# One token turn per tick, gains and rows asked for later, and two token operands of the FFN cut one product later

## The chip, the cores and the metric

The kernel runs on one core of one Trainium2 chip. The time is the device time of one launch in microseconds, the median of three runs. Its engines are named as the profile names them: PE (TensorE, matmuls), PEld (TensorE's weight loads), DVE (VectorE), ACT (ScalarE), POOL (GpSimd), SP (SyncE, which issues nearly all DMAs here). Each engine works through its own instructions in the order of the program and waits for the others by semaphores.

## What is computed

One layer of a decoder on 2048 tokens of 1024 float32 values (one batch): gated linear attention beside a short gated convolution, then a SwiGLU FFN of 2816 hidden values, then a gate over a per-token embedding, each behind an RMS norm and added to the residual `h`.

```python
u = _rmsnorm(h, ln1_g[i])
proj = u @ w_in[i]
q, k, v, g, g_lr, cb, cc, cx = jnp.split(proj, offsets, axis=-1)
...
mix = jnp.concatenate([o, y], axis=-1) @ w_out[i]
h = h + mix
u2 = _rmsnorm(h, ln2_g[i])
a, bb = jnp.split(u2 @ w_gate_upffn[i], 2, axis=-1)
h = h + (jax.nn.silu(a) * bb) @ w_down[i]
u3 = _rmsnorm(h, ln3_g[i])
gate = jax.nn.sigmoid(u3 @ w_ple_gate[i])
h = h + gate * (p[i] @ w_ple_proj[i])
...
return _rmsnorm(h, lnf_g)
```

`o` is the normed and gated result of the attention, `y` that of the convolution.

## The kernel before

**Number form.** A float32 operand is split into a high part (an ACT cast to fp32r) and a low part (a DVE subtraction of the high part from the source); `split_into` (L176 to L179) writes both. A product takes three matmuls for each pair of operands (high by high, high by low, low by high: `PASSES`). So each operand that comes from memory passes a DMA, an ACT cast and a DVE subtraction before PE can use it.

**Seven products for eight.** The FFN's two matmul stages and the gate of the embedding cut their matrices into 2 by 2 blocks and make seven block products in place of eight, from sums and differences of blocks. `ORDER` (1, 6, 2, 5, 7, 3, 4) is the order in which they run. The operands of the seven products (token side and weight side) are made once, stored to DRAM and loaded when their turn comes.

**Stages.** `mixing_phase` (0 to some 930 us) works on four blocks of 512 tokens: input projection, attention, convolution, output projection. The end of a block overlaps with the start of the next. Each token tile of 128 tokens is normed (`normed`: ACT squares, POOL `ms` and `rs`, DVE L212) and then *turned*: eight 128x128 PE transposes (L219) in two halves, each half into one of two PSUM banks named `tr`. There are two kinds of turn. `norm_to` turns a tile of the next block's input and splits each half into uT (ACT L178, DVE L179), and both must have read a bank before it is free. `norm_to_ops` turns a tile of the finished block for the FFN; ACT copies the halves out (L250), DMAs store them, and for blocks 1 and 3 POOL also subtracts (L234) to make operands 4 to 7.

**What sets the order around a turn.** The turns are put in a list with a due time by `later`; `tick` (L143) runs between products, and once inside a long product, and runs all entries that are due. PE's order follows from that. DVE's, ACT's and POOL's orders in this stage are made by a scheduler from the same program.

**The up stage** (`up_phase`, some 930 to 1806 us): two halves of 1024 tokens by 11 pairs of hidden chunks by seven products. `go(n, ...)` runs product n for two 128-row tiles of weights `wu` against a token operand `U[b][n]`, ticks after each tile and takes one entry of the list `side`. The token operands stay for all 11 pairs; they are loaded by `fetch_U` (L292: two DMAs into `ur`, and two cuts, each an ACT cast and a DVE subtraction into U). In the first pair the operands of products 3 and 4, the last two, are asked for after the first and second product, and their cuts go into `side` at once. The instructions of all engines are issued in the order written. `done5` adds the accumulated product to `u2` on DVE (L234 is the helper's line).

**The last phase** (`last_phase`, from some 1806 us): `down` for each half b of the tokens, then `gated` for each. `stream` (L1070) runs a product in steps of 12 matmuls; each job of two steps loads a weight operand `wr` and a token operand `mr` (`load`, L1044) and cuts them into `wh` and `mh` two jobs ahead; `load(x + 4)` is four jobs ahead. `then(n, fn)` runs `fn` n steps later. `rows_of` asks for the eight rows (`h`, 512 KB each) of the residual `h_mid`, three at once and five at step 12. `gain_of` loads a norm's gain vector to all partitions. After product 3 and 4 of `down`, each token tile is normed, turned (L1123), copied by ACT (L1124), subtracted on POOL and stored by SP (L1177) for the gate stage.

Of the kernel before, what the change touches and what calls it, by code (L numbers as in the profile page):

```python
# [19 lines left out]
NT = T // P  # L20
# [10 lines left out]
ORDER = (1, 6, 2, 5, 7, 3, 4)  # L31
GLA_WAIT = 10
EQ = 2
N1, N2, N3 = 7, 3, 3
LEVELS = (128, 64, 32, 16, 8, 4)
NL = len(LEVELS)

# [2 lines left out]
def hybrid_layer(ctx: ExitStack, tc: tile.TileContext,  # L40
# [100 lines left out]
    side = [None]  # L141

    def tick():  # L143
        clock[0] += 1
        while queue and queue[0][0] <= clock[0]:
            queue.pop(0)[1]()
        if side[0] is not None and next(side[0], "end") == "end":
            side[0] = None

# [1 line left out]
        while queue:  # L151
            queue.pop(0)[1]()

    def later(n, fn):
        queue.append((clock[0] + n, fn))
        queue.sort(key=lambda e: e[0])

    PASSES = ((0, 0), (0, 1), (1, 0))
# [63 lines left out]
    def norm_to(src, u, ti, gain, delay):  # L222
        xn = normed(src, gain)

        def transposes():
            for kk in range(2):
                tp = transposed(xn, kk)
                split_into(u[kk][:, :, 0, ti * P:(ti + 1) * P], u[kk][:, :, 1, ti * P:(ti + 1) * P], tp)
        if delay is None:
            return transposes  # L230
        later(delay, transposes)

    def tensor(e, out, a, b, op):
        return e.tensor_tensor(out=out, in0=a, in1=b, op=op)  # L234
# [1 line left out]
    def norm_to_ops(src, tile, ops, gain, delay):  # L236

        xn = normed(src, gain)  # L240
        tok = tok_of(tile % NT)
        old = w4([P, 2, 4, P]) if tile >= NT else None
        if tile >= NT:
            for kk in range(2):
                nc.sync.dma_start(out=old[:, kk], in_=ops[1 + kk][:, :, tok])

        def transposes():
            ut = w4([P, 2, 4, P])
            for kk in range(2):
                nc.scalar.copy(out=ut[:, kk], in_=transposed(xn, kk))  # L250
            put = lambda n, t: nc.sync.dma_start(out=ops[n][:, :, tok], in_=t)
            if tile < NT:
                put(1, ut[:, 0])
                put(2, ut[:, 1])
                return
            put(3, ut[:, 1])
            s = w4([P, 2, 4, P])
            g = nc.gpsimd
            tensor(g, s[:, 0], ut[:, 0], old[:, 0], ALU.subtract)
            put(5, s[:, 0])  # L260
            tensor(g, s[:, 1], ut[:, 1], s[:, 0], ALU.subtract)
            put(6, s[:, 1])
            tensor(g, ut[:, 0], ut[:, 1], ut[:, 0], ALU.subtract)
            put(7, ut[:, 0])
            tensor(g, old[:, 1], old[:, 1], s[:, 1], ALU.subtract)
            put(4, old[:, 1])
        later(delay, transposes)

    def load_x(b, ti, eng, gate=None):
        xt = w4([P, D])  # L270
# [521 lines left out]
    def up_phase(st):  # L792
# [137 lines left out]
        for b in range(NBB):  # L930
            for i in range(NPR):
                bk = {}
                s0 = 7 * (b * NPR + i)

                def go(n, on, done):

                    g = s0 + ORDER.index(n)
                    run(g)
                    w = W.pop(g)
                    bk[n] = [mm_bank() for _ in range(2)] if on is None else bk[on]  # L940
                    for e in range(2):
                        product(bk[n][e], lambda k, s: w[:, s, k, e * P:(e + 1) * P],
                                lambda k, s: U[b][n][:, k, s, :], 4, start=on is None, skip_group_check=True)
                        done(e, bk[n][e])
                        tick()
                        if side:
                            side.pop(0)()
                    if b == 0 and i == 0 and n in ORDER[:2]:
                        side.extend(fetch_U(0, ORDER[5 + ORDER.index(n)]))
                    if b + 1 < NBB and i == NPR - 1:  # L950
                        side.extend(fetch_U(b + 1, n))
                u2, b2, m1, m2 = [None] * 2, [None] * 2, [None] * 2, [None] * 2

                def done1(e, x):
                    u2[e] = v2()
                    nc.scalar.copy(out=u2[e], in_=x)  # L956

                def done2(e, x):
                    m1[e] = v2()
                    nc.scalar.activation(out=m1[e], in_=x, func=AF.Silu)  # L960

                def done5(e, x):
                    b2[e] = v2()
                    add(b2[e], x, u2[e])

                def done3(e, x):
                    m2[e] = v2()
                    add(m2[e], x, u2[e])
                    nc.scalar.activation(out=m2[e], in_=m2[e], func=AF.Silu)

                def done4(e, x):
                    add(u2[e], x, u2[e])
                    tensor(V, m2[e], m2[e], b2[e], ALU.mult)
                    tensor(V, m1[e], m1[e], u2[e], ALU.mult)
                go(1, None, done1)
                go(6, None, lambda e, x: add(u2[e], x, u2[e]))
                go(2, 1, done2)
                go(5, None, done5)
                go(7, None, lambda e, x: add(b2[e], x, b2[e]))
                go(3, 5, done3)  # L980
                go(4, 7, done4)

                put = lambda n, x, b=b, i=i: nc.sync.dma_start(out=hid_ops[b][n][:, i, :], in_=x)

                def plain(m1=m1, m2=m2, put=put):
                    put(1, m1[0])
                    put(2, m1[1])
                    put(3, m2[1])

                def sums(m1=m1, m2=m2):  # L990
                    sub(m1[0], m2[0], m1[0])
                    sub(m2[0], m2[1], m2[0])
                    sub(m2[1], m2[1], m1[0])
                    sub(m1[1], m1[1], m2[1])

                def summed(m1=m1, m2=m2, put=put):
                    put(5, m1[0])
                    put(7, m2[0])
                    put(6, m2[1])
                    put(4, m1[1])  # L1000
                at(s0 + 8, 3, plain)
                at(s0 + 8, 4, sums)
                at(s0 + 10, 3, summed)
# [5 lines left out]
    def last_phase(st):  # L1009
# [141 lines left out]
            then(start + gap[1], scale)  # L1151
            last_fn(got)

        def down(b, g3):
            h = rows_of(h_mid, b, 12)
            acc = [v("acc") for _ in range(NT)]
            bk = {}
            second = [None] * NT
# [8 lines left out]

            def complete(t, turn_at, fn):
                then(1, lambda: nc.sync.dma_start(out=h_out[b * 2 * NT + t], in_=h[t]))
                norm_steps(h[t], g3, 2 * (t % NT), (1, 3), lambda got: then(turn_at, lambda: fn(t % NT, got["xn"])))  # L1170

            def later_half(t, xn):
                second[t] = turn(xn, "ut")
# [41 lines left out]
        def rows_of(src, b, wait):  # L1215
# [4 lines left out]
                h[t] = pl["h"].tile([P, D], F32, name="h")  # L1220
                nc.sync.dma_start(out=h[t], in_=src[b * 2 * NT + t])
            for t in range(2 * NT):
                if t < 3:
                    load_row(t)
                else:
                    then(wait, lambda t=t: load_row(t))
            return h

        def gated(b, lnf, final):
# [160 lines left out]

        for x in range(3):
            load(x)
        g3, lnf = gain_of(ln3_g[0]), gain_of(lnf_g)
        cut(0)
        load(3)
        cut(1)
        for b in range(NBB):
            down(b, g3)
        gated(0, lnf, False)
        gated(1, lnf, True)  # L1400

# [41 lines left out]
```

## Time and profile before

| | |
|---|---|
| median of 3 runs | 2440.58 us (2438.98 to 2441.0) |
| profiled execution, its own time | 2438.52 us |
| its span on the core | 2436.8 us |
| mean granted TensorE clock | 0.992 |
| instructions | 31370 |
| TensorE busy | 2366.4 us, 97% of the span |
| VectorE, ScalarE, GpSimd busy | 57%, 40%, 29% |
| DMA | 470.02 MB, mean 193 GB/s |

The span is what the profiler saw on the core, the execution's own time lies 1.7 us above it. A matmul's end is modelled, so PE rows overlap a little; the start of the next row is the surer number. `x24` at the end of a row stands for 24 instructions of that form in sequence.

### The profile page before, as it was taken

Reading aid. Unit: us, or ns where it says so; the run is one execution under the profiler, and the core shown is the slowest. Engines: PE = TensorE matmul, PEld = TensorE weight load, DVE = VectorE, ACT = ScalarE, POOL = GpSimd, SP = SyncE. Lnnn points to the kernel's source line nnn. Section 1 sums busy time; section 2 is a strip of 40 time slices with the busy share of each in tenths; the row PEclk is TensorE's granted clock in tenths of the full one; section 3 lists DMA queues with packets and bytes.
Section 4 is the critical chain, followed back from the end, with each engine's and each line's share of the span. In section 5 each row is a group of like instructions: output and inputs, shape, how many; then the busy total and the mean of one; then the engine's idle time right before and its main releaser. Section 6 shows DMA issues by size and latency. Waiting matters only on the chain.

```text
span 2436.8 us, 31370 instructions
## 1 busy us (share of the span) xinstructions
PE 2366.4 (97%) x11752; PEld 1940.5 (80%) x11752; DVE 1401.1 (57%) x1674; ACT 972.9 (40%) x1531; POOL 713.7 (29%) x604
## 2 busy tenths in 40 slices
PE   7999999999999999999999999999999999999995
PEld 6777878787887787788888888888878888788774
DVE  4765475566547643655555754544446555756777
ACT  4434433453345335322222522222224344435556
POOL 3401220430104014343434144245432005301522
PEclk9999999999999999999999999999999999999998
DMA  5225423742442259644545676567757669866997
GB/s 166 78 70 192 116 84 130 219 128 67 160 147 78 70 191 332 232 160 139 173 149 182 218 255 216 183 222 255 263 208 274 198 221 293 286 194 229 323 330 285
DMA packets 302888, 470.02 MB, mean 193 GB/s; under 512 B 22656, under 2 KB 187024, under 8 KB 302736
## 3 DMA queue, kind: packets, MB, share of 16 engines
q1 hardware_dynamic: 300240, 459.61, 56.2%
q0 software_dynamic: 2496, 8.41, 1.4%
q8 instruction: 92, 1.51, 0.3%
q14 instruction: 60, 0.49, 0.1%
HBM read 325.87 MB, written 142.08 MB: 192 GB/s over the span
## 4 chain that ended last, share of the span: by engine, by line
PE 67%; DMA 5%; DVE 3%; issue 2%; ACT 2%; POOL 1%; SPq 1%; POOLq 0%; DVEq 0%; ACTq 0%
PE mm L164 48%; PE ps L1090 16%; DMA mr<-hid 1%; DMA ur<-up 1%; PE g L444 1%; DVE mh L179 1%; DMA pp<-emb 1%; DMA wr<-wp 1%; POOL as L234 1%; DMA mr<-u 1%; DMA out_dram<-w 1%; DVE h L234 0%; DMA wr<-in_w_ple_gate_dram 0%; PE ps L1123 0%; SPq L815 0%
## 5 line engine op out<-in xcount | busy, mean ns | idle before, releaser
L1090 PE MATMUL ps<-wh,mh 128*128 128x512 f32 x2496 | 578.0, 392 | 13.1 <-ACT mh L178 7.5
L1090 PEld LDWEIGHTS ps<-wh,mh 128*128 128x128 f32 x2496 | 468.7, 189 | 116.1 <-ACT mh L178 10.5
L164 PE MATMUL mm<-uT,wu 128*128 128x512 f32 x2112 | 482.9, 389 | 0.3 <-ACT v L956 0.2
L164 PE MATMUL mm<-uT,hl 128*128 128x512 f32 x1920 | 472.1, 400 | 0.0
L164 PEld LDWEIGHTS mm<-uT,wu 128*128 128x128 f32 x2112 | 396.2, 188 | 83.4 <-ACT v L956 0.6
L164 PEld LDWEIGHTS mm<-uT,hl 128*128 128x128 f32 x1920 | 353.8, 188 | 87.7 <-issue 2.6
L164 PE MATMUL mm<-U,wu 128*128 128x512 f32 x1584 | 364.5, 390 | 4.1 <-DVE v L234 4.1
L164 PEld LDWEIGHTS mm<-U,wu 128*128 128x128 f32 x1584 | 298.4, 188 | 66.7 <-issue 4.5
L179 DVE TENSOR_TENSOR wu<-raw,wu 128x1024 fp32r<-128x1024 f32 x154 | 217.7, 1414 | 208.1 <-ACT wu L178 208.1
L178 ACT CAST wu<-raw 128x1024 fp32r<-128x1024 f32 x154 | 161.4, 1049 | 303.8 <-PE mm L164 227.1
L164 PE MATMUL mm<-hl,uT 128*128 128x512 f32 (+1 forms) x1488 | 278.6, 346 | 3.4 <-DVE uT L179 2.1
L179 DVE TENSOR_TENSOR wh<-wr,wh 128x1024 fp32r<-128x1024 f32 x111 | 142.1, 1280 | 217.2 <-ACT wh L178 215.5
L164 PEld LDWEIGHTS mm<-hl,uT 128*128 128x128 f32 x1488 | 234.8, 190 | 39.1 <-DVE uT L179 2.7
L234 DVE TENSOR_TENSOR v<-mm,v 128x512 f32<-128x512 f32 x220 | 151.0, 688 | 154.9 <-PE mm L164 154.0
L234 POOL TENSOR_TENSOR v<-v,v 128x512 f32<-128x512 f32 x88 | 140.8, 1600 | 301.3 <-DMA hid<-v 285.4
L178 ACT CAST wh<-wr 128x1024 fp32r<-128x1024 f32 x111 | 110.8, 998 | 248.3 <-PE ps L1090 179.0
L234 POOL TENSOR_TENSOR raw<-raw 128x1024 f32<-128x1024 f32 x44 | 106.0, 2419 | 210.5 <-issue 152.7
L179 DVE TENSOR_TENSOR mh<-mr,mh 128x1024 fp32r<-128x1024 f32 x111 | 145.2, 1308 | 8.2 <-ACT mh L178 7.7
L179 DVE TENSOR_TENSOR hl<-raw,hl 128x512 fp32r<-128x512 f32 x160 | 118.6, 765 | 49.2 <-ACT hl L178 49.0
L178 ACT CAST hl<-raw 128x512 fp32r<-128x512 f32 x160 | 93.8, 618 | 73.9 <-PE mm L164 62.5
L178 ACT CAST mh<-mr 128x1024 fp32r<-128x1024 f32 x111 | 110.6, 996 | 14.3 <-DMA mr<-hid 7.5
L234 POOL TENSOR_TENSOR ur<-ur 128x512 f32<-128x512 f32 x60 | 93.2, 1553 | 31.3 <-DMA ur<-in_w_ple_gate_dram 27.9
(194 smaller groups left out, 2059.8 us busy)
## 6 DMA issues: line engine op xcount, KB each, us to landing
raw<-in_w_gate_upffn_dram SPq DMA_DIRECT2D x77, 512.0 KB, 4.6
hid<-v SPq DMA_DIRECT2D x154, 256.0 KB, 3.7
mr<-hid SPq DMA_DIRECT2D x70, 512.0 KB, 4.7
raw<-in_w_in_dram SPq DMA_DIRECT2D x64, 512.0 KB, 3.8
wu<-raw SPq DMA_DIRECT2D x44, 512.0 KB, 2.8
raw<-wu SPq DMA_DIRECT2D x44, 512.0 KB, 5.8
wr<-wd SPq DMA_DIRECT2D x40, 512.0 KB, 3.8
w<-in_x_dram SPq DMA_DIRECT2D x32, 512.0 KB, 8.4
```

Source lines behind the costliest of these rows:

```text
L164: nc.tensor.matmul(out=out_ap, lhsT=lhs(k, a), rhs=rhs(k, b), start=(start and k == 0 and i == 0), stop=(k == nk - 1 and i == 2), **kw)
L178: nc.scalar.copy(out=hi, in_=src)
L179: nc.vector.tensor_tensor(out=lo, in0=src, in1=hi.bitcast(F32), op=ALU.subtract)
L234: return e.tensor_tensor(out=out, in0=a, in1=b, op=op)
L444: nc.tensor.matmul(out=sp[par][:, a, :], lhsT=X[r, c], rhs=X[r, c], start=True, stop=True)
L1090: nc.tensor.matmul(out=bk[n][t], lhsT=M[a][:, j, tok_of(t)], rhs=W[c][:, j, :], start=(on is None and k == 0 and i == 0), stop=(k == nk - ...
```

## The change

It makes four edits.

- **Turns.** Entries of the tick's list carry a mark. Of the marked ones (both kinds of turn) only one runs in a tick; the others that are due wait for the next. `N2`, the delay of one kind, goes from 3 to 4.
- **Token operands of the up stage.** Product 3's operand is still asked for after product 1, but its cuts go into `side` only after product 6; product 4's is asked for after product 2 in place of 6, and cut after product 5.
- **Gains.** The two gain vectors of the last phase are asked for at its steps 16 and 24, not ahead of its fourth load.
- **Rows.** The rows of the first `down` are asked for at steps 3, 4, 5 and then 13 to 17, one each; those of the second at steps 10 to 17.

```diff
--- before.py
+++ after.py
@@ -31,7 +31,7 @@
 ORDER = (1, 6, 2, 5, 7, 3, 4)
 GLA_WAIT = 10
 EQ = 2
-N1, N2, N3 = 7, 3, 3
+N1, N2, N3 = 7, 4, 3
 LEVELS = (128, 64, 32, 16, 8, 4)
 NL = len(LEVELS)
 
@@ -141,9 +141,14 @@
     side = [None]
 
     def tick():
+
         clock[0] += 1
-        while queue and queue[0][0] <= clock[0]:
-            queue.pop(0)[1]()
+        turned = False
+        for e in [e for e in queue if e[0] <= clock[0]]:
+            if not (e[2] and turned):
+                queue.remove(e)
+                e[1]()
+                turned = turned or e[2]
         if side[0] is not None and next(side[0], "end") == "end":
             side[0] = None
 
@@ -151,8 +156,8 @@
         while queue:
             queue.pop(0)[1]()
 
-    def later(n, fn):
-        queue.append((clock[0] + n, fn))
+    def later(n, fn, turns=False):
+        queue.append((clock[0] + n, fn, turns))
         queue.sort(key=lambda e: e[0])
 
     PASSES = ((0, 0), (0, 1), (1, 0))
@@ -228,7 +233,7 @@
                 split_into(u[kk][:, :, 0, ti * P:(ti + 1) * P], u[kk][:, :, 1, ti * P:(ti + 1) * P], tp)
         if delay is None:
             return transposes
-        later(delay, transposes)
+        later(delay, transposes, True)
 
     def tensor(e, out, a, b, op):
         return e.tensor_tensor(out=out, in0=a, in1=b, op=op)
@@ -264,7 +269,7 @@
             put(7, ut[:, 0])
             tensor(g, old[:, 1], old[:, 1], s[:, 1], ALU.subtract)
             put(4, old[:, 1])
-        later(delay, transposes)
+        later(delay, transposes, True)
 
     def load_x(b, ti, eng, gate=None):
         xt = w4([P, D])
@@ -945,8 +950,10 @@
                         tick()
                         if side:
                             side.pop(0)()
-                    if b == 0 and i == 0 and n in ORDER[:2]:
-                        side.extend(fetch_U(0, ORDER[5 + ORDER.index(n)]))
+                    if b == 0 and i == 0 and n in (ORDER[0], ORDER[2]):
+                        cuts[:] = fetch_U(0, ORDER[5 + ORDER.index(n) // 2])
+                    elif b == 0 and i == 0 and n in (ORDER[1], ORDER[3]):
+                        side.extend(cuts)
                     if b + 1 < NBB and i == NPR - 1:
                         side.extend(fetch_U(b + 1, n))
                 u2, b2, m1, m2 = [None] * 2, [None] * 2, [None] * 2, [None] * 2
@@ -1151,8 +1158,8 @@
             then(start + gap[1], scale)
             last_fn(got)
 
-        def down(b, g3):
-            h = rows_of(h_mid, b, 12)
+        def down(b):
+            h = rows_of(h_mid, b, 10)
             acc = [v("acc") for _ in range(NT)]
             bk = {}
             second = [None] * NT
@@ -1167,7 +1174,7 @@
 
             def complete(t, turn_at, fn):
                 then(1, lambda: nc.sync.dma_start(out=h_out[b * 2 * NT + t], in_=h[t]))
-                norm_steps(h[t], g3, 2 * (t % NT), (1, 3), lambda got: then(turn_at, lambda: fn(t % NT, got["xn"])))
+                norm_steps(h[t], gains["g3"], 2 * (t % NT), (1, 3), lambda got: then(turn_at, lambda: fn(t % NT, got["xn"])))
 
             def later_half(t, xn):
                 second[t] = turn(xn, "ut")
@@ -1220,10 +1227,7 @@
                 h[t] = pl["h"].tile([P, D], F32, name="h")
                 nc.sync.dma_start(out=h[t], in_=src[b * 2 * NT + t])
             for t in range(2 * NT):
-                if t < 3:
-                    load_row(t)
-                else:
-                    then(wait, lambda t=t: load_row(t))
+                then(wait + t if t > 2 or b > 0 else 3 + t, lambda t=t: load_row(t))
             return h
 
         def gated(b, lnf, final):
@@ -1390,14 +1394,16 @@
 
         for x in range(3):
             load(x)
-        g3, lnf = gain_of(ln3_g[0]), gain_of(lnf_g)
+        gains = {}
+        then(16, lambda: gains.update(g3=gain_of(ln3_g[0])))
+        then(24, lambda: gains.update(lnf=gain_of(lnf_g)))
         cut(0)
         load(3)
         cut(1)
         for b in range(NBB):
-            down(b, g3)
-        gated(0, lnf, False)
-        gated(1, lnf, True)
+            down(b)
+        gated(0, gains["lnf"], False)
+        gated(1, gains["lnf"], True)
```

What that does to the instructions shows at three places. Numbers behind names are buffer numbers. Line numbers of the changed kernel are some 5 to 7 higher for the same statement (L219 becomes L224, L164 becomes L169).

The first is PE at the boundary from the first mixing block to the second. `w_1935`, `w_1971` and `w_2007` are tiles of the next block's input, `w_2088`, `w_2137` and `w_2201` tiles of the finished block. Before:

```order
L219 MATMUL tr<-ident,w_1935 128x128 x8
L164 MATMUL mm<-hl,uT 128x512 x24
L219 MATMUL tr<-ident,w_1971 128x128 x8
L219 MATMUL tr<-ident,w_2088 128x128 x8
L164 MATMUL mm<-hl,uT 128x512 x24
L219 MATMUL tr<-ident,w_2007 128x128 x8
L219 MATMUL tr<-ident,w_2137 128x128 x8
L164 MATMUL mm<-hl,uT 128x512 x24
L219 MATMUL tr<-ident,w_2201 128x128 x8
```

And in the changed kernel:

```order
L224 MATMUL tr<-ident,w_1935 128x128 x8
L169 MATMUL mm<-hl,uT 128x512 x24
L224 MATMUL tr<-ident,w_1971 128x128 x8
L169 MATMUL mm<-hl,uT 128x512 x12
L224 MATMUL tr<-ident,w_2088 128x128 x8
L169 MATMUL mm<-hl,uT 128x512 x12
L224 MATMUL tr<-ident,w_2007 128x128 x8
L169 MATMUL mm<-hl,uT 128x512 x12
L224 MATMUL tr<-ident,w_2137 128x128 x8
L169 MATMUL mm<-hl,uT 128x512 x12
L169 MATMUL mm<-hl,uT 128x264 x24
L224 MATMUL tr<-ident,w_2201 128x128 x8
```

Twice two turns stood behind one another; now half a product of 12 matmuls stands between them, and the later turns of the finished block come a tick later. The other boundaries change in the same way.

The second is DVE in the first pair of the up stage, from the products 5 and 7 on. U2_8572 (U2_8644 after) is the operand of product 4, U2_8530 (U2_8563 after) that of product 3; `v2_8612<-mm_8598` (`v2_8607<-mm_8593` after) and the row that follows are the adds of `done5`. Before:

```order
L234 TENSOR_TENSOR v2_8483<-mm_8515,v2_8483 128x512
L179 TENSOR_TENSOR U2_8530<-ur_8504,U2_8530 128x2x512
L234 TENSOR_TENSOR v2_8500<-mm_8516,v2_8500 128x512
L179 TENSOR_TENSOR U2_8530<-ur_8506,U2_8530 128x2x512
L179 TENSOR_TENSOR wu_8552<-raw_8248,wu_8552 128x1024
L179 TENSOR_TENSOR U2_8572<-ur_8548,U2_8572 128x2x512
L179 TENSOR_TENSOR U2_8572<-ur_8550,U2_8572 128x2x512
L179 TENSOR_TENSOR wu_8591<-raw_8250,wu_8591 128x1024
L234 TENSOR_TENSOR v2_8612<-mm_8598,v2_8483 128x512
L234 TENSOR_TENSOR v2_8626<-mm_8599,v2_8500 128x512
L179 TENSOR_TENSOR wu_8628<-raw_8511,wu_8628 128x1024
L234 TENSOR_TENSOR v2_8612<-mm_8634,v2_8612 128x512
```

And in the changed kernel:

```order
L239 TENSOR_TENSOR v2_8483<-mm_8515,v2_8483 128x512
L239 TENSOR_TENSOR v2_8500<-mm_8516,v2_8500 128x512
L184 TENSOR_TENSOR wu_8543<-raw_8248,wu_8543 128x1024
L184 TENSOR_TENSOR U2_8563<-ur_8504,U2_8563 128x2x512
L184 TENSOR_TENSOR U2_8563<-ur_8506,U2_8563 128x2x512
L184 TENSOR_TENSOR wu_8586<-raw_8250,wu_8586 128x1024
L239 TENSOR_TENSOR v2_8607<-mm_8593,v2_8483 128x512
L239 TENSOR_TENSOR v2_8621<-mm_8594,v2_8500 128x512
L184 TENSOR_TENSOR wu_8623<-raw_8511,wu_8623 128x1024
L239 TENSOR_TENSOR v2_8607<-mm_8629,v2_8607 128x512
L184 TENSOR_TENSOR U2_8644<-ur_8582,U2_8644 128x2x512
L239 TENSOR_TENSOR v2_8621<-mm_8630,v2_8621 128x512
```

Both operands' subtractions stood ahead of the adds of `done5`; now product 3's stand there, and product 4's begin behind them.

The third is SP where the up stage ends and the last phase begins. `hid1_...<-v2` are stores of the up stage's results, `wr` and `mr` the loads of the last phase's jobs, `h` its rows. Before:

```order
L1044 DMA mr_14315<-hid0_1_130 128x1024
L983 DMA hid1_1_137<-v2_14094 128x512
L1020 DMA gain_14317<-in_ln3_g_dram 128x1024
L1020 DMA gain_14319<-in_lnf_g_dram 128x1024
L983 DMA hid1_2_139<-v2_14108 128x512
L983 DMA hid1_3_142<-v2_14206 128x512
L983 DMA hid1_5_140<-v2_14094 128x512
L983 DMA hid1_7_141<-v2_14191 128x512
L1044 DMA wr_14327<-in_w_down_dram 128x2x512
L983 DMA hid1_6_138<-v2_14206 128x512
L983 DMA hid1_4_143<-v2_14108 128x512
L1044 DMA mr_14329<-hid0_1_130 128x1024
```

And in the changed kernel:

```order
L1051 DMA mr_14315<-hid0_1_130 128x1024
L1051 DMA wr_14323<-in_w_down_dram 128x2x512
L1051 DMA mr_14325<-hid0_1_130 128x1024
L1051 DMA wr_14341<-in_w_down_dram 128x2x512
L1051 DMA mr_14343<-hid0_1_130 128x1024
L990 DMA hid1_1_137<-v2_14094 128x512
L1051 DMA wr_14375<-in_w_down_dram 128x512
L1051 DMA mr_14377<-hid0_1_130 128x512
L990 DMA hid1_2_139<-v2_14108 128x512
L990 DMA hid1_3_142<-v2_14206 128x512
L990 DMA hid1_5_140<-v2_14094 128x512
L990 DMA hid1_7_141<-v2_14191 128x512
```

Two jobs' loads moved ahead of the first of these stores, and the next job's behind that store; the gains are gone from here and the rows come after the stores.

## The prediction

> **What bounds the kernel now.** I read the busy time of each engine first, then the waits of TensorE grouped by what they wait for, then the timeline at each of those waits.
>
> ```profile
> PE 2366.4 (97%) x11752; PEld 1940.5 (80%) x11752; DVE 1401.1 (57%) x1674; ACT 972.9 (40%) x1531; POOL 713.7 (29%) x604
> ```
>
> TensorE is busy 97% of the span, so whatever the change does to another engine counts only where TensorE stands still because of it. The seven largest waits below are 42.4 us together; 10.3 of it, the first row, is the start of the program, which the change doesn't reach.
>
> ```profile
> PE tr L219 <- DVE w L212: 10.3, 1, 10.3
> PE ps L1090 <- ACT mh L178: 7.5, 5, 2.2
> PE tr L219 <- ACT w L250: 6.4, 7, 1.6
> PE tr L219 <- DVE uT L179: 6.4, 6, 1.3
> PE ps L1090 <- DVE mh L179: 5.4, 8, 1.7
> PE mm L164 <- DVE v L234: 4.1, 1, 4.1
> PE mm L164 <- ACT v L921: 2.3, 1, 2.3
> ```
>
> Columns: who waits on what, us in total, how often, the longest. The reader is to see that the waits fall into three kinds: transposes (L219) that wait for a PSUM bank (6.4 and 6.4 us), the last phase's matmuls (L1090) that wait for token operands (7.5 and 5.4), and one wait of 4.1 in the FFN up stage. The change edits something near each. Behind a wait come two further losses: the matmul pipeline drains and refills, and sometimes the granted clock halves for a while.
>
> **Part 1, one turn per tick.** At the three boundaries between mixing blocks two turns stand back to back, twice each:
>
> ```profile
> 224.58 1.04 PE L219 MATMUL tr<-ident,w 128*128 128x128 f32 x8
> 226.58 0.66 PE L219 MATMUL tr<-ident,w 128*128 128x128 f32 x4 [0.97 <-DVE uT L179]
> 227.97 0.66 PE L219 MATMUL tr<-ident,w 128*128 128x128 f32 x4 [0.73 <-ACT w L250]
> 228.38 5.87 PE L164 MATMUL mm<-hl,uT 128*128 128x512 f32 x24
> 234.08 1.04 PE L219 MATMUL tr<-ident,w 128*128 128x128 f32 x8
> ```
>
> Columns: start, us, engine, line, operation, count, and in brackets the idle time ahead and what ended it. Four transposes take 0.41 (227.97 to 228.38), so sixteen need 1.64, and the pair took 3.80 (224.58 to 228.38). It loses 2.16: gaps of 0.97 and 0.73, and 0.46 for two refills, 0.23 each. In all the two kinds of wait are 12.8 us in 13 gaps (the waits table), with 13 refills of 0.23 that is 15.8. One pair costs more:
>
> ```profile
> 451.73 7.09 PE L164 MATMUL mm<-hl,uT 128*128 128x512 f32 x24
> 458.65 1.03 PE L219 MATMUL tr<-ident,w 128*128 128x128 f32 x8
> ```
>
> These 24 matmuls took 6.92 up to the next row, where 24 of the same form took 5.70 in the fence above (228.38 to 234.08): 1.2 for a lowered clock. So **17.0 us** is what part 1 could bring at most.
>
> It won't bring all. After the change half a product, 12 matmuls or 2.85 us, stands between the two turns of a pair, but the second still needs the bank that the first leaves. VectorE empties it in this order:
>
> ```profile
> 237.35 1.28 DVE L212 SCALAR_TENSOR_TENSOR w<-w,rs,w 128x1024 f32<-128x1024 f32 x1 [1.32 <-POOL rs L199]
> 238.55 0.68 DVE L179 TENSOR_TENSOR uT<-tr,uT 128x512 fp32r<-128x512 f32 x1
> ```
>
> The low-part subtraction that frees the second bank (L179) stands behind the normalization of the next token tile (L212, which waits for ScalarE's squares and GpSimd's rs) and ends at 239.23, 5.15 after its turn began at 234.08. That order stays. With the change the second turn's second half comes up after 0.82 + 2.85 + 0.41 = 4.08. It waits 1.1, with a refill 1.3 in place of 2.16, six times: 5.0 saved. Added to that: the pairs that are worse than this one, 15.8 - 6 x 2.16 = 2.8 (the largest single gap, 1.6, is a lone turn that waits for ScalarE copies and moves later), and the 1.2 of clock. Against it: a transpose of the gate's low-rank input now comes right behind a turn and must wait for the copy of its bank, a ScalarE copy or two, which I estimate at 0.5 with refill, three times, 1.5; and at the second boundary GpSimd's subtractions for the odd block beside VectorE's, which I take at 1.5 (the nearest row is the 1.2 to 1.6 by which that boundary is already worse). Sum: 5.0 + 2.8 + 1.2 - 1.5 - 1.5 = **6.0 saved**; ends 0, if every wait moves one turn further, and 12.
>
> [...]
>
> The last block's turns also come one tick later. Their results feed the up stage through memory, and its first wait (ACT v L921, 2.3 in the table) hangs on such a load. Bounds: 0 and 1.5 slower, about half a product; I take **0.5 lost**.
>
> **Part 2, U operands cut later.** This is the wait of 4.1:
>
> ```profile
> 988.16 1.22 DVE L179 TENSOR_TENSOR U<-ur,U 128x1024 fp32r<-128x1024 f32 x1 [1.44 <-ACT U L178]
> 989.98 1.23 DVE L179 TENSOR_TENSOR U<-ur,U 128x1024 fp32r<-128x1024 f32 x1 [0.60 <-ACT U L178]
> 991.13 1.22 DVE L179 TENSOR_TENSOR wu<-raw,wu 128x1024 fp32r<-128x1024 f32 x1
> 992.26 1.28 DVE L234 TENSOR_TENSOR v<-mm,v 128x512 f32<-128x512 f32 x2
> ```
> ```profile
> 993.09 12.76 PE L164 MATMUL mm<-U,wu 128*128 128x512 f32 x48 [4.14 <-DVE v L234]
> 1005.69 21.92 PE L164 MATMUL mm<-uT,wu 128*128 128x512 f32 x96
> ```
> ```profile
> 993.74:997.15 3.41, 3.41 (x10) 2.63 (x9) 3.11 (x3) 0.00 (x0) 3.33 (x2) 0.50 0.39 154
> ```
>
> VectorE runs in order. Its adds of `done5` (992.26), whose banks product 3 needs, stand behind two subtractions on the last operand U, which wait for ScalarE's casts and those for the transfer (idle 1.44 and 0.60). Then the clock is 0.50 for a whole window of 3.41. The 48 matmuls took 12.60 (993.09 to 1005.69); at the pace of the next row, 21.92 for 96 or 0.228 each, 10.96: 1.6 more. With the gap and a refill 4.14 + 0.23 + 1.6 = 6.0.
>
> In the new order the `done5` adds come ahead of that operand's subtractions (the order of VectorE above this prediction). What is late next is the operand itself, for product 4:
>
> ```profile
> 983.88 0.34 SPq L297 DMA_DIRECT2D ur<-up  x1
> ```
>
> It was issued at 983.88 and the second half's subtraction began at 989.98. It is now asked for one product later, but SyncE was behind already, so I put its landing 1 to 3 us later: subtraction done by 992 to 994. Product 3 can start at 993.09 - 4.14 = 988.95 and takes half of 10.96, so product 4 needs it at 994.4. That leaves some 0.4 to 2.4. **5.8 saved**; ends 2.0 (it is late by 2.4 and costs a refill and a clock window of 1.6) and 6.0.
>
> **Part 3, gains not ahead of the first loads.** SyncE at the start of the last phase:
>
> ```profile
> 1805.60 0.33 SPq L1020 DMA_DIRECT2D gain<-in_ln_g_dram  x1
> 1805.99 1.98 SPq L1020 DMA_DIRECT2D gain<-in_lnf_g_dram  x1
> ...
> 1817.61 0.38 SPq L1044 DMA_DIRECT2D mr<-hid  x1
> ```
> ```profile
> 1823.55 0.73 PE L1090 MATMUL ps<-wh,mh 128*128 128x512 f32 x2 [1.70 <-ACT mh L178]
> 1824.81 5.99 PE L1090 MATMUL ps<-wh,mh 128*128 128x512 f32 x24 [0.53 <-DVE mh L179]
> ```
>
> The second gain's issue alone holds SyncE 1.98; the fourth job's token operand (mr) was issued only at 1817.61, behind the gains and six stores of the up stage. TensorE then waited 1.70 and 0.53, and 0.52 once more (the row of VectorE's mh has 8 such waits). In the new order two jobs stand ahead of the first of those stores, and the gains are at steps 16 and 24. Three gaps and three refills: 2.75 + 0.69 = 3.4, **3.4 saved**. Ends 0 (the transfers are bound by bandwidth: job 4 and 5 now compete) and 3.4. At steps 16 and 24 the two gains add 1 MB to a stretch in which the timeline shows no TensorE gap, and their first user is the normalization after product 3: nothing.
>
> **Part 4, rows one per step.** At the second `down`, TensorE loses:
>
> ```profile
> 2051.20 1.06 PE L1123 MATMUL ps<-ident,w 128*128 128x128 f32 x8 [1.28 <-DVE w L1147]
> 2052.02 22.05 PE L1090 MATMUL ps<-wh,mh 128*128 128x512 f32 x96
> 2076.17 0.74 PE L1090 MATMUL ps<-wh,mh 128*128 128x512 f32 x2 [2.10 <-ACT mh L178]
> 2077.43 4.84 PE L1090 MATMUL ps<-wh,mh 128*128 128x512 f32 x20 [0.52 <-DVE mh L179]
> ```
> ```profile
> 2026.73 2.97 SPq L1221 DMA_DIRECT2D h<-h_mid  x3
> ```
> ```profile
> 2038.68 1.05 ACT L178 CAST mh<-mr 128x1024 fp32r<-128x1024 f32 x1 [0.48 <-DMA mr<-hid]
> 2039.64 1.06 ACT L1124 COPY as<-ps 128x512 f32<-128x512 f32 x2
> ```
> ```profile
> 2036.75 1.03 PE L1123 MATMUL ps<-ident,w 128*128 128x128 f32 x8
> ```
>
> Three rows of 0.5 MB were asked for at 2026.73, ahead of the loads whose mr ended ScalarE's wait at 2038.68. That cast stands ahead of the copies of a turn (2039.64). The turn took 1.03 from 2036.75, so the copies came 1.9 late, and GpSimd's subtractions behind them set when SyncE, which issues in order, can store and then load: the mr that TensorE misses at 2076.17. The same chain holds the normalization that 2051.20 waits for.
>
> Without the three rows there the chain starts up to 1.9 earlier. One row, of step 10, still comes ahead of the last stores. Gaps 1.28 + 2.10 + 0.52 and refills 0.69 are 4.6; a shift of 1.9 takes all of the first (1.5), most of the second (1.9 of 2.3) and perhaps the third (half, 0.4); less 0.5 for the row: **3.3 saved**. Ends: 1 lost and 4.6 saved. In the first `down` rows come at steps 3 to 5 and 13 to 17 in place of 0 and 12, first used after step 12: nothing.
>
> **Sum.** 6.0 - 0.5 + 5.8 + 3.4 + 3.3 = 18.0 saved. The profiled execution took 2438.5: 2420.5. The median of the runs is 2440.6, 2.1 above it, so the same saving gives 2422.6, **2423**.
>
> **Rivals.**
>
> - The boundaries bring nothing. For it: the subtraction that frees the bank depends on the normalization, and that on ScalarE and GpSimd, so the wait may follow the turn however far it stands. Against: 2.85 us of matmuls are put between. Time: 2422.6 + 6.0 = 2428.6.
> - Product 4 takes over product 3's wait. For it: the margin of 0.4 to 2.4 rests on my estimate of a landing. Time: 2422.6 + 3.8 = 2426.4. With the first rival: 2432.4.
> - Everything behind the waits shifts freely (12 in part 1, all ends): 18.0 + 6.0 + 0.5 + 0.2 + 1.3 is 26.0, so 2414.6.
> - The other side: the eight rows of the second `down` stand each ahead of a load pair in a stretch that is full:
>
> ```profile
> 2052.00:2078.00 26.00, 23.37 (x103) 18.72 (x102) 12.39 (x9) 10.65 (x14) 11.69 (x7) 1.00 1.07 347
> ```
>
> The DMA engines are busy 1.07 here at 347 GB/s, so a row of 0.5 MB is 1.5 us of everything behind it. Rows at steps 10 to 17 with jobs of 1 MB every two steps (5.5 us) ask for 2 MB or 6.0 us in 5.5, beside stores that still drain. If the jobs' reserve is used up when step 10 comes, eight rows push the loads by 12 us, and four resulting gaps at 1.6 of lowered clock add 6.4; part 4's 3.3 is gone. That is 21.7 on the forecast: 2444.3. It decides once a load takes longer than the two jobs, 11 us, by which it is asked ahead of its cut; the five rows asked for at once before came behind the critical load and made no gap.
>
> **How the numbers follow.** Forecast 0.50; boundaries bring nothing 0.16; product 4 waits 0.13; both 0.07; all shifts freely 0.08; rows make loads late 0.06. The likeliest gives 2423. The range goes down to 2414, and up to 2433 with both milder rivals. What a measurement of this kernel can tell from no change is about 0.2%, 4.9 us, so faster means below 2435.7. The first five cases are faster, 0.94, but the last of them to the slow side leave 3 us, and a partial backlog may eat it: faster 0.87, same 0.08, slower 0.05.
>
> **What would show it.** Part 1: TensorE's rows of 8 transposes stand apart, with a gap of about 1.1 on VectorE's uT at every second one; no gap at all would make it too small. Part 2: no row of 4 us near 990; a new gap on U near 994 is the second rival. Part 3: no waits for mh near 1823. Part 4: no gap at 2076, that at 2051 smaller; if loads of mr in 2050 to 2100 take over 11 us, the last rival holds. The prediction is wrong if these seven waits of TensorE, 42.4 us, don't fall below 34 (half of the 18.0 as gaps).

## The result, and the profile after

The changed kernel took 2425.35 us, median of 4 runs (2424.2 to 2427.48), the one before 2439.78 in the same comparison: a ratio of 0.9935 with a 95% interval of 0.9923 to 0.9947. The forecast was 2423, in a range of 2414 to 2433. The profiled execution took 2425.30, 13.2 less than that of before (2438.52). One execution of a later version, the one with the operands' edit alone, ran at a mean clock of 0.752 and took 2941.38; it is left out below.

The page's busy time of the engines first, and then the waits of TensorE in the changed kernel (columns as before: us in total, how often, the longest):

```profile
PE 2361.1 (97%) x11752; PEld 1938.5 (80%) x11752; DVE 1407.3 (58%) x1674; ACT 972.1 (40%) x1531; POOL 718.1 (30%) x604
```

```profile
PE tr L224 <- DVE w L217: 10.3, 1, 10.3
PE tr L224 <- DVE uT L184: 7.2, 6, 2.0
PE ps L1097 <- ACT mh L183: 6.8, 5, 2.6
PE ps L1097 <- DVE mh L184: 5.5, 8, 1.7
PE mm L169 <- ACT v L926: 3.3, 1, 3.3
...
PE ps L1130 <- DVE w L1154: 1.4, 2, 1.3
...
PE mm L169 <- DVE hl L106: 1.1, 1, 1.1
```

The wait of 4.1 on `done5` is gone, and so is the one of the turns on ScalarE's copies. What stays is the turns' wait on uT (6.4 before, 7.2 now) and about the same waits for token operands. The first wait of the up stage grew from 2.3 to 3.3. The seven waits of the prediction are 33.1 in all, from 42.4, just below the 34 that it set as its limit (42.4 less half of the 18.0 is 33.4); two new kinds, on VectorE's hl (1.1) and of the low-rank transposes (0.8), are not among them.

To see where the 13.2 came from I took the same matmul, counted from the start of the program, in both traces and subtracted its start times. The difference changes only at a few places:

| stretch | forecast, us | measured, us |
|---|---|---|
| start of the program (to 60) | 0 | -1.1 |
| three block boundaries | -6.0 | -4.2 (-1.3, -3.5, +0.6) |
| start of the up stage (945 to 985) | +0.5 | +1.0 |
| products 3 and 4 of the up stage (993) | -5.8 | -6.0 |
| start of the last phase (1815 to 1840) | -3.4 | -3.9 |
| second `down` (2040 to 2090) | -3.3 | +1.5 |
| gate stage and tail | 0 | -0.5 |
| sum | -18.0 | -13.2 |

At the boundary of the first two blocks, TensorE's timeline of the changed kernel reads:

```profile
227.19 0.60 PE L224 MATMUL tr<-ident,w 128*128 128x128 f32 x4
228.88 0.66 PE L224 MATMUL tr<-ident,w 128*128 128x128 f32 x4 [1.09 <-DVE uT L184]
229.30 3.05 PE L169 MATMUL mm<-hl,uT 128*128 128x512 f32 x12
232.19 1.04 PE L224 MATMUL tr<-ident,w 128*128 128x128 f32 x8
232.98 3.04 PE L169 MATMUL mm<-hl,uT 128*128 128x512 f32 x12
```

The first turn is off to itself, 12 matmuls follow, and the second turn's first half runs at once (227.19). Its second half waits 1.09 for VectorE, in the size that the prediction gives. At the third boundary the same wait is longer and the matmuls behind it are slow:

```profile
673.80 0.86 PE L224 MATMUL tr<-ident,w 128*128 128x128 f32 x4 [1.98 <-DVE uT L184]
674.31 4.50 PE L169 MATMUL mm<-hl,uT 128*128 128x512 f32 x12
678.65 0.60 PE L224 MATMUL tr<-ident,w 128*128 128x128 f32 x4
```

Twelve matmuls took 4.34 there (674.31 to 678.65) and 2.89 above (229.30 to 232.19), 1.45 more. The cause is the granted clock:

```profile
674.12:677.52 3.40, 3.40 (x12) 2.72 (x10) 0.00 (x0) 0.59 (x1) 0.00 (x0) 0.50 0.42 121
950.60:957.41 6.81, 5.52 (x13) 4.37 (x14) 4.91 (x4) 3.96 (x6) 0.42 (x1) 0.50 0.66 205
2063.34:2066.74 3.40, 3.40 (x9) 2.62 (x10) 2.23 (x2) 2.09 (x2) 0.00 (x0) 0.50 1.02 402
```

The number behind the five engines' busy times is the clock: 0.50 in each of these three stretches. The first and the third were at full clock before; the second, the start of the up stage, was low for 3.4 us and now is for 6.8. In exchange the low stretches of before at 24, 451, 994, 2359 and 2380 are gone; those at 24, 2359 and 2380 lie where the change does nothing.

### The profile page after: what moved, and what is told of

Its sections match the earlier page's. It is cut to its first block, busy times and chain, and to the rows that moved or that the text cites. A ratio compares the mean times of both kernels' runs of the same rounds, so it can differ in the third digit from the quotient of the medians.

```text
span 2423.6 us, 31366 instructions
## 1 busy us (share of the span) xinstructions
PE 2361.1 (97%) x11752; PEld 1938.5 (80%) x11752; DVE 1407.3 (58%) x1674; ACT 972.1 (40%) x1531; POOL 718.1 (30%) x604
## 5 line engine op out<-in xcount | busy, mean ns | idle before, releaser
L169 PE MATMUL mm<-uT,wu 128*128 128x512 f32 x2112 | 482.4, 389 | 0.0
L169 PE MATMUL mm<-uT,hl 128*128 128x512 f32 x1920 | 472.1, 400 | 0.0
L169 PEld LDWEIGHTS mm<-uT,wu 128*128 128x128 f32 x2112 | 396.8, 188 | 82.3
L169 PEld LDWEIGHTS mm<-uT,hl 128*128 128x128 f32 x1920 | 353.8, 188 | 87.7 <-issue 2.6
L169 PE MATMUL mm<-U,wu 128*128 128x512 f32 x1584 | 362.6, 389 | 0.0
L169 PEld LDWEIGHTS mm<-U,wu 128*128 128x128 f32 x1584 | 297.4, 188 | 61.6
L184 DVE TENSOR_TENSOR wu<-raw,wu 128x1024 fp32r<-128x1024 f32 x154 | 223.4, 1451 | 203.1 <-ACT wu L183 203.1
L169 PE MATMUL mm<-hl,uT 128*128 128x512 f32 (+1 forms) x1488 | 278.9, 346 | 4.5 <-DVE uT L184 2.1
L169 PEld LDWEIGHTS mm<-hl,uT 128*128 128x128 f32 x1488 | 233.3, 189 | 40.2 <-DVE uT L184 2.7
```

What stands on the lines that cost most here:

```text
L169: nc.tensor.matmul(out=out_ap, lhsT=lhs(k, a), rhs=rhs(k, b), start=(start and k == 0 and i == 0), stop=(k == nk - 1 and i == 2), **kw)
L184: nc.vector.tensor_tensor(out=lo, in0=src, in1=hi.bitcast(F32), op=ALU.subtract)
```

## The experiments

**Each edit alone.** Four kernels have one edit of the change each, on the kernel before. The first has the turns:

```diff
-N1, N2, N3 = 7, 3, 3
+N1, N2, N3 = 7, 4, 3
...
+            if not (e[2] and turned):
+                queue.remove(e)
+                e[1]()
+                turned = turned or e[2]
...
```

> The kernel before with the turns' edit alone (one turn per tick, N2 = 4). My theory: the six pairs leave one wait each on VectorE's uT (0.9 to 2.0 us, about 7 in all) in place of 12.8 us of waits, and the last block's later turns make the first wait of the up stage longer (3.3 in place of 2.3). About 4 us saved at the boundaries, 1 lost near 950, each lowered clock window adding or taking 1.7: ratio 0.9975 to 1.000. Rival (the boundaries bring nothing): the waits on the bank add up to over 11 us again and the ratio is at or above 1.000.

It took 2436.47 against 2442.84 of the kernel before in the same comparison, ratio 0.9971 (0.9960 to 0.9982). Its waits on the bank are six, on VectorE's uT, 0.93 to 1.52 each; the difference to the kernel before across the three boundaries is 6.1 us, more than the 4.2 of the changed kernel, where a low clock window at the third boundary cost 1.45; none fell low here. The first wait of the up stage is 3.15. So the edit saves at the boundaries what the sum says, 2 more than the 4 expected of this version, and the start of the up stage is 0.8 slower.

The second has the up stage's operands:

```diff
-                    if b == 0 and i == 0 and n in ORDER[:2]:
-                        side.extend(fetch_U(0, ORDER[5 + ORDER.index(n)]))
+                    if b == 0 and i == 0 and n in (ORDER[0], ORDER[2]):
+                        cuts[:] = fetch_U(0, ORDER[5 + ORDER.index(n) // 2])
+                    elif b == 0 and i == 0 and n in (ORDER[1], ORDER[3]):
+                        side.extend(cuts)
```

> The kernel before with the up stage's operands alone (asked for and cut later). My theory: the gap of 4.1 near 990 and its lowered clock window go and no gap on U takes their place: 6 us saved, 2434 to 2436, ratio about 0.9975. Rival (product 4 takes the wait over): a gap of 1 to 3 us on U some 10 us later, ratio 0.999 or above.

It took 2434.70 (median of four, 2433.26 to 2438.46), ratio 0.9968 (0.9953 to 0.9983). The same kernel was profiled once more:

> A second look at the up stage's operands alone, for a profile at full clock. My theory: no gap of TensorE over 0.5 us between 975 and 1010 (4.14 before), some 6 us saved there. Rival: a gap of 1 to 3 us on U near 994.

One run, 2436.45. The waits of TensorE between 960 and 1010 in this trace:

```profile
PE mm L164 <- ACT v L921: 1.6, 1, 1.6
```

The only wait belongs to the start of the stage (965.9); neither the old one nor the rival's is there. The difference to the kernel before grows by 6.0 at this place.

The third has the gains:

```diff
-        g3, lnf = gain_of(ln3_g[0]), gain_of(lnf_g)
+        gains = {}
+        then(16, lambda: gains.update(g3=gain_of(ln3_g[0])))
+        then(24, lambda: gains.update(lnf=gain_of(lnf_g)))
...
```

> The kernel before with the gains alone moved to steps 16 and 24. If the gains ahead of the fourth load were the cause of the three gaps at 1823 to 1831 (2.75 us together), these go and 3 to 4 us are saved: 2436 to 2437. Rival: the three residual rows, which this kernel still asks for at step 0 between the fourth and the fifth job, are the cause of the last two gaps (0.53 and 0.52), so that one gap of 0.5 or two stay and at most 2.5 us are saved.

It took 2440.4, ratio 0.9987 (0.9978 to 0.9997). At the start of the last phase the difference to the kernel before falls by 3.2, and one gap of 0.32 is left of 2.75. The gains were the main cause. What the last gap hangs on isn't shown: in the changed kernel, with the rows moved too, no gap is left and 3.9 are saved, but the version with the rows taken back (below) saves 3.9 there as well, with three rows still asked for at step 0.

The fourth has the rows:

```diff
-            h = rows_of(h_mid, b, 12)
+            h = rows_of(h_mid, b, 10)
...
-                if t < 3:
-                    load_row(t)
-                else:
-                    then(wait, lambda t=t: load_row(t))
+                then(wait + t if t > 2 or b > 0 else 3 + t, lambda t=t: load_row(t))
```

> The kernel before with the rows alone asked for one per step. The theory on record (rows hold up the second down): gaps of 1.28 and 2.10 near 2051 and 2076 shrink, 3 us saved there. The theory after seeing the changed kernel's trace (GpSimd's chain of subtractions sets both, whatever the rows do): gaps of 1.2 to 1.3 and 1.9 to 2.2 stay there, 0 saved, or 1.6 lost if the clock falls behind the second. At 1823 the rows alone leave the first gap of 1.7.

It took 2438.92, ratio 0.9986 (0.9976 to 0.9995). The waits of TensorE in its second `down`, from 2000 to 2100:

```profile
PE ps L1123 <- DVE w L1147: 1.4, 2, 1.3
PE ps L1090 <- ACT mh L178: 1.4, 1, 1.4
PE ps L1090 <- DVE mh L179: 0.5, 1, 0.5
```

The normalization's wait is what it was. That for mr fell from 2.1 to 1.4, so the theory on record gets 0.7 of its 3.3. 1.6 were saved at the start of the last phase, where this kernel's gaps are 1.15 and 0.53 in place of 1.70, 0.53 and 0.52; I had expected that the first stays at 1.7.

**The rows taken back.** This is the changed kernel without the edit to the rows (the diff above, reversed).

> The changed kernel with the rows asked for as before (three at once and five at step 12). If GpSimd's chain sets the second down's waits, they stay at 1.2 to 1.3 and 1.9 to 2.4 there, and the total changes by no more than a clock window (1.7 us). By the theory on record, that the rows hold the stage up, removing the edit costs about 3 us there. Rows at step 0 may bring back one gap of 0.3 to 0.5 near 1820.

One run, 2426.08, within the changed kernel's own runs (2424.2 to 2427.48). Waits of TensorE from 2000 to 2100, first of this kernel and then of the changed one:

```profile
PE ps L1097 <- ACT mh L183: 1.9, 1, 1.9
PE ps L1130 <- DVE w L1154: 1.3, 1, 1.3
PE ps L1097 <- DVE mh L184: 0.5, 1, 0.5
```

```profile
PE ps L1097 <- ACT mh L183: 2.0, 1, 2.0
PE ps L1130 <- DVE w L1154: 1.4, 2, 1.3
PE ps L1097 <- DVE mh L184: 0.5, 1, 0.5
```

They agree to 0.1. Where the rows are asked for is worth nothing there. The gaps that I feared near 1820 didn't come back either: with the gains gone, three rows at step 0 do no harm, and 3.9 are saved at the start of the last phase as in the changed kernel.

**GpSimd relieved.** In the changed kernel, two of the four subtractions per token tile after product 4 of the first `down` go to VectorE:

```diff
-                sub(b2[:, 0], b2[:, 1], b2[:, 0])
+                tensor(V if b == 0 else G, b2[:, 0], b2[:, 1], b2[:, 0], ALU.subtract)
...
-                sub(s4, a[:, 1], s[:, 1])
+                tensor(V if b == 0 else G, s4, a[:, 1], s[:, 1], ALU.subtract)
```

> The changed kernel with two of GpSimd's four subtractions per tile of the first down's last product given to VectorE. My theory (GpSimd's chain, 32 us for four tiles, sets the normalization that TensorE waits for at 2037 and the stores and loads behind them): both gaps, 1.28 and 2.02 with 0.52, fall by more than half, 2 to 5 us saved. Rival (the DMA engines, busy 1.0 to 1.06 there, set it): the first gap goes, since it hangs on rs alone, but the second stays at 1.7 or above.

One run, 2421.12. Waits of TensorE in the same stretch:

```profile
PE ps L1130 <- DVE w L1154: 0.7, 1, 0.7
PE ps L1097 <- DVE mh L184: 0.4, 1, 0.4
```

Of 3.98 (the four gaps at 2029, 2037, 2062 and 2063 of the changed kernel) 1.15 are left, and no clock window falls low there. The difference to the kernel before moves by 3.0 in the right direction, where it moved by 1.5 in the wrong one in the changed kernel: 4.5 gained. The rival, that the full DMA engines (busy 1.00 and 1.06 between 2012 and 2064 in the changed kernel) set the second gap, falls: they carry the same transfers here, and the loads of mr in this stretch still take up to 10.3 from issue to landing (10.4 in the changed kernel). GpSimd's work on the four tiles, from its first subtraction to its last, takes 24.2 here and 31.9 in the changed kernel.

**Turns further apart.** In the changed kernel, the finished block's turns come three ticks later at the first three boundaries, so that 24 matmuls or more stand between any two turns:

```diff
-                            norm_to_ops(h[ti], (b % 2) * NT + ti, up_ops[b // 2], g2, N2 if more else N2 + 2)
+                            norm_to_ops(h[ti], (b % 2) * NT + ti, up_ops[b // 2], g2, N2 + 3 if more else N2 + 2)
```

> The changed kernel with the finished block's turns three ticks later at the first three boundaries (N2 + 3 for all blocks but the last), so that at least 24 matmuls, 5.7 us, stand between any two turns of the boundary. My theory (the bank is freed some 5.2 us after a turn begins, since the subtraction stands behind the next tile's normalization): the six waits on uT, 7.2 us with 1.4 of refills, go, and 6 to 8.5 us are saved if nothing else waits. Rival (the wait follows the turn, since the normalization hangs on the tile before it): the waits on uT or on ScalarE's copies add up to over 5 us again and nothing is saved. A third way: later turns collide with the low-rank transposes (0.28 each, up to 1 in all).

It took 2412.73 (2412.52 to 2414.74), ratio 0.9890 (0.9873 to 0.9908). The boundary of the first two blocks:

```profile
230.86 1.04 PE L224 MATMUL tr<-ident,w 128*128 128x128 f32 x8
231.66 5.86 PE L169 MATMUL mm<-hl,uT 128*128 128x512 f32 x24
237.35 1.04 PE L224 MATMUL tr<-ident,w 128*128 128x128 f32 x8
238.14 6.10 PE L169 MATMUL mm<-hl,uT 128*128 128x264 f32 x48
244.08 1.04 PE L224 MATMUL tr<-ident,w 128*128 128x128 f32 x8
```

No row has a wait, at this or at the other two boundaries, and the low-rank transposes don't wait either (no gap above 0.25). Across the three boundaries the difference to the kernel before is 17.1, beside a bound of 17.0 in the prediction. The first rival is out: the wait doesn't follow the turn however far it stands. In the changed kernel the six waits end 5.2 to 6.3 after the turn ahead began (223.51 to 228.88 in the first), and here the next turn begins 6.5 after it (230.86 to 237.35).

The 12.9 between 4.2 and 17.1 is more than the 6 to 8.5 expected. It is all that was still lost at the boundaries: the waits on uT 7.2 with 1.4 of refills, the wait on hl 1.3 and the low-rank transposes 1.5, refills included, and the lowered clock 1.45.

**The last block's turns as before.**

```diff
-                            norm_to_ops(h[ti], (b % 2) * NT + ti, up_ops[b // 2], g2, N2 if more else N2 + 2)
+                            norm_to_ops(h[ti], (b % 2) * NT + ti, up_ops[b // 2], g2, N2 if more else N2 + 1)
```

> The changed kernel with the last block's turns one tick earlier, as before the change. My theory: the first wait of the up stage falls from 3.3 back to some 2.3 and its lowered clock from 6.8 us to 3.4, so 1 to 2.5 us are saved near 950. Rival (that wait is set by the transfers there, which run at full DMA share, not by the turns): the gap stays at 3.0 to 3.5.

One run, 2428.86. The gap is 2.77, between the two expectations, the clock is low for 6.8 behind it as in the changed kernel, and the stretch from 945 to 985 costs 0.76 against 1.0. TensorE's turns and GpSimd's subtractions of the last block stand as before the change again, and yet the wait isn't 2.3. The tick is at most a part of it. Nor is it the lowered clock: in the six traces without a low window there TensorE waits a second time instead, 1.4 to 1.6. What else makes the up stage's start 0.3 to 1.0 slower in all seven profiles with the turns' edit, and not in three without it, stays open.

**Both improvements.** The turns further apart and GpSimd relieved, together:

> The changed kernel with the finished block's turns three ticks later at the first three boundaries and two of GpSimd's four subtractions per tile on VectorE in the first down's last product. If the two gains are of different places and add up, 12.6 and some 4 us below the changed kernel: 2407 to 2410, ratio 0.986 to 0.988. Rival: what VectorE takes over, or the earlier end, makes the gate stage's loads late: 2411 or more.

It took 2410.23 (2408.39 to 2410.6), ratio 0.9873 (0.9857 to 0.9889): the ratio that was expected, and 0.2 above the expected 2407 to 2410. Up to 2250 the difference to the kernel before is 30.1; 1.6 are given back in the gate stage and the tail, where one clock window falls low at 2259 and loads wait as they did. It is the fastest version of this study, 15 below the changed kernel.

## Why the prediction was right, and where it was not

**Sign and size hold, with 4.8 us of difference in the profiled execution.** Three of the five terms are within 1 us of their forecast; part 1 fell 1.8 short and part 4 failed by 4.8. The total is nearer than that by luck: 1.6 of the 13.2 come from the start and the tail, where the forecast had nothing and the change does nothing. The term for the last block's turns, 0.5 lost, measured 1.0; with these turns a tick earlier it is still 0.8, so its cause stays open.

**Part 1** gave 4.2 of 6.0. The residual waits were forecast as 1.1 each; they are 0.93 to 1.98. The mechanism, a bank that is freed 5.2 us or more after its turn begins since the subtraction stands behind the next normalization, is shown by the version with the turns further apart, in which all six go. The wait of 1.07 on hl at 466 is GpSimd's subtractions beside VectorE's (1.5 in the forecast): VectorE's five cuts of hl took 7.55 beside them, and 3.17 at the first boundary, which has none. The low-rank transposes cost 0.28 each plus a refill, as forecast. What the step missed is the clock: it counted one lowered window going, but with gaps of about 2 us left, a window at the third boundary fell low, 1.45. The version with the turns alone had none there and saved 6.1.

**Part 2** gave 6.0 of 5.8. `done5` ahead of the late operand's cuts is enough; the rival, that product 4 waits in its place, is refuted in the changed kernel and with that edit alone. (The low end of 2.0 in the prediction is 1.8 by its own terms, 6.0 less 2.4, 0.23 and 1.6.)

**Part 3** gave 3.9 of 3.4. The gains alone give 3.2 and the rows alone 1.6, which overlap: with the gains gone from there the rows add nothing, since the version with the rows taken back gives 3.9 too.

**Part 4** is the step that failed: "Without the three rows there the chain starts up to 1.9 earlier." The copies of the second turn did come earlier, 0.6 after it began in place of 2.9 (2036.75 to 2039.64 in the prediction's lines), as they no longer stood behind a late cast:

```profile
2022.57 1.03 PE L1130 MATMUL ps<-ident,w 128*128 128x128 f32 x8
2023.20 1.07 ACT L1131 COPY as<-ps 128x512 f32<-128x512 f32 x2 [1.11 <-PE ps L1130]
```

But GpSimd had hardly waited for them. Its rows of before, from the first tile's subtractions to the last of the fourth tile's, and then those of the changed kernel:

```profile
2031.71 3.77 POOL L234 TENSOR_TENSOR as<-ut,as 128x512 f32<-128x512 f32 x2 [1.80 <-ACT as L1124]
2035.44 1.29 POOL L234 TENSOR_TENSOR ut<-ut 128x512 f32<-128x512 f32 x1
2036.69 1.29 POOL L234 TENSOR_TENSOR x<-as 128x512 f32<-128x512 f32 x1
...
2040.29 4.07 POOL L234 TENSOR_TENSOR as<-ut,as 128x512 f32<-128x512 f32 x2 [0.41 <-ACT as L1124]
...
2062.48 1.29 POOL L234 TENSOR_TENSOR x<-as 128x512 f32<-128x512 f32 x1
```

```profile
2017.53 3.77 POOL L239 TENSOR_TENSOR as<-ut,as 128x512 f32<-128x512 f32 x2 [1.80 <-ACT as L1131]
2021.27 2.27 POOL L239 TENSOR_TENSOR ut<-ut 128x512 f32<-128x512 f32 x1
2023.50 2.27 POOL L239 TENSOR_TENSOR x<-as 128x512 f32<-128x512 f32 x1
...
2048.17 1.28 POOL L239 TENSOR_TENSOR x<-as 128x512 f32<-128x512 f32 x1
```

From the first subtraction to the last it took 32.1 before (2031.71 to 2063.77) and 31.9 after (2017.53 to 2049.45). Its idle time ahead of the second tile was 0.41, the most that earlier copies could give back, and the first tile's last two subtractions grew by more: 1.29 became 2.27 each. VectorE's rows in the same stretch of the changed kernel:

```profile
2021.17 1.23 DVE L184 TENSOR_TENSOR wh<-wr,wh 128x1024 fp32r<-128x1024 f32 x1 [2.39 <-ACT wh L183]
2022.32 2.30 DVE L184 TENSOR_TENSOR mh<-mr,mh 128x1024 fp32r<-128x1024 f32 x1
```

And VectorE's next row in the kernel before:

```profile
2038.23 1.23 DVE L179 TENSOR_TENSOR wh<-wr,wh 128x1024 fp32r<-128x1024 f32 x1 [5.27 <-ACT wh L178]
```

It had been idle for 5.27 there, while GpSimd made those two subtractions, because the late operand wasn't cast. With the rows out of the way it made its cuts while GpSimd subtracted, and the two slowed each other. So GpSimd bound the chain in both kernels, and the transfers that I took for its cause only decided when VectorE would disturb it. To take a start for the cause of an end, one has to see that the engine between is idle at some point; here the timeline of before showed GpSimd idle for 0.41 and busy from 2040 on, and I had read it. That the stage is then 1.5 slower is a clock window and no longer wait: the gaps are 3.98 in place of 3.90.

**The rivals.** The other side (rows that make loads late, 2444) didn't come: the loads of mr behind the rows made no new gap, and between 2050 and 2100 none took more than 10.4 from issue to landing, below the 11 that was to decide it. That rows alone change so little either way is the same finding.

**The clock.** In the changed kernel a window fell low behind a gap of 1.98 at the third boundary. The sum lacked a measure of its own for when that happens; the traces of the two kernels give one, in the last section.

## What to carry to other kernels

Two uses of a ring of PSUM banks need a distance in time, not only something between them: read off when the last reader leaves the bank (here the waits ended 5.2 to 6.3 us after the turn ahead began), and put at least that much work between (with 6.5 no wait was left). An engine that works in order and waits for late data holds back what stands behind it: VectorE's two subtractions that waited 1.44 and 0.60 for the late operand stood ahead of the adds for which TensorE waited 4.14. So put the work that someone waits for ahead of the work whose data comes late. Before a transfer is named as the cause of a late chain, see whether the engine that works through the chain is idle anywhere in it; if it is idle only briefly, an earlier start buys no more than that.

## What the hardware showed

**When the clock falls.** In the traces of the kernel before and of the changed one the clock falls and rises on a grid of 3.41 us: all its changes in one trace lie whole multiples of that apart (from 24.35 to 2417.09 before, from 674.11 to 2404.67 after), and the grid is at another phase in each (0.46 and 1.69 from the first instruction). In both I added up TensorE's gaps in each window of the grid, from 100 us on and up to 2380, leaving out windows that were low already. After each of 7 windows with 1.9 us or more of gaps (1.98 to 2.77), the next was at 0.50; after none of 19 with 0.9 to 1.65; in between it was 1 of 3 (1.81, and not 1.70 and 1.87). A low window was followed by a second one once, where it held 1.29 of gaps itself (at 951, after), and by full clock in eight cases, where it held 0.05 or less. So a gap of 1.21 and one of 0.97 in one window were enough (447.60 to 451.02, before), and the low window behind them cost 1.2 (at 451, before); the one at 994, before, cost 1.6. Gaps of 2.10 and 0.52 that the grid divided into 1.70 and 0.93 were followed by no low window (2072.35 to 2079.17, before), and 2.02 and 0.52 in one window were followed by one (at 2063, after). So what such gaps cost hung on where the grid lay. Two or three low windows more or less, at 1.2 to 1.6 each, are by my estimate as much as the 1 to 4 us between single runs of one kernel, though that was not followed run by run.

**Two engines at half speed.** A subtraction of 128x512 on GpSimd took 1.29 with VectorE idle (2035.44, before) and 2.27 beside VectorE's subtractions of 128x1024 (2021.27, after). Of these the first, begun 0.10 ahead of GpSimd's, took 1.23, as one did beside GpSimd's 128x1 operations alone (2038.23, before), and the second 2.30 (rows above). Each that was slowed grew by about 1.0, a little under one instruction of the other. What makes them slow each other is not shown.
